# A decoder layer on one core: the embedding's projection moves from expert 19 to behind the last expert

## The chip, the cores and the metric

The kernel runs on one core of a Trainium2 chip. The metric is the device time of one execution in microseconds (us); the median of three runs is 1429.41 us (1429.36 to 1429.43).

## The reference, cut to what matters

One decoder layer on 512 tokens of width 1024, all in float32. A mixing sublayer is followed by a mixture of 32 experts, of which each token takes four, and by the part that the change is about: a per-layer embedding `p` of width 256 is projected to 1024, gated by a sigmoid of a 1024x1024 linear map of the residual, and added ahead of the last normalisation.

```python
x = layer_norm(DEEPNORM_ALPHA * x + ffn, ln2_g[i], ln2_b[i])          # ffn: the experts' output
gate = jax.nn.sigmoid((x @ ple_gate_w[i] + ple_gate_b[i]).astype(jnp.float32)).astype(x.dtype)
ple = p[i] @ ple_proj[i]
x = layer_norm(DEEPNORM_ALPHA * x + gate * ple, ln3_g[i], ln3_b[i])
```

`ple` depends on the inputs alone, so it can be computed at any time before the last loop.

## The kernel before

**Weights in chunks.** All weights pass through one list of chunks of 1 MB (`add`), in the order of use: for each expert eight chunks of its gate and up matrices, then four of the down matrix of the expert before. The chunk of `ple_proj` (`c_pp`) stands behind those of expert 19 (`EMBED + 1`), the four of `ple_gate_w` (`c_pg`) at the end. A ring of 14 buffers holds them. `load` brings a chunk into a free buffer by SP's queue; `split` makes two parts of it, a rounded one (`hi`, a cast on ScalarE, L114) and the rest (`lo`, a subtraction on VectorE, L117), so that each product is three matmuls (`mm3`, L210 to L212). `ahead(j)` says that chunk j is used: `done` gives its buffers back and loads what fits, `splits` splits the next chunks, up to three ahead of the one in use. `limit` says how far the list may be loaded; until the last expert it is two gate chunks short of the end.

**The experts.** The order of instructions on every engine is the order of the program text (it is written out by hand). In the loop over `e`, TensorE takes the eight chunks k = 0 to 7 of the expert (12 matmuls each), and then the four down chunks of the expert before (`down(e - 1)`), 12 each. Behind chunk 2 it transposes the hidden values of the expert before (`split_t`, L307), behind chunk 7 the gathered tokens of the next one. A transposition writes to a small PSUM buffer `tr`, of which there are two, taken in turn; ScalarE copies it out (L322) and VectorE subtracts (L323), and then the buffer is free again. `emit` scales the output and adds it to `acc` in DRAM by an indirect DMA from GpSimd (POOL), the scatter.

**Steps between chunks.** Generators are advanced behind given chunks: `embed_parts` in expert 19 behind chunks 1, 3, 4, 5 and 6 (first the two parts of the gate's bias, `pgb`, then for each of four tiles of `p` two transposes into a `tr` buffer, a copy on ScalarE and a subtraction on VectorE, L841 to L843), and `prepare` in expert 31 behind the same chunks (first the two parts of `b_down`, `bd`, then one transpose and one ScalarE copy for each tile, into `gt_`). `embed()` stands behind expert 19's down chunks: four tiles of 12 matmuls of 512 columns into `big`, a PSUM tile of which there are three, and a ScalarE copy of each to `ple[i]` (L853).

**The end.** Behind the last expert's `down`, whose output is halved between ScalarE and VectorE (L351, L352), come the remaining splits, 10 matmuls that only keep TensorE busy (`keep_warm`), and a loop of further blocks for experts with more than 96 tokens (`further_blocks`). It runs zero times here, but at its head all engines wait until each of them and the scatter are done (L768). Then SP loads the sum from `acc` (L999), two `combine` tiles add the experts' bias (L1011), 14 more `keep_warm` matmuls run, and for each of four tiles of tokens there is a normalisation (`second`), a transposition (`turn2`), the gate (`gate`, L1035 to L1042), the product with `ple` and the last normalisation.

Of the kernel before, what the change touches and what calls it, by code (L numbers as in the profile page):

```python
# [20 lines left out]
P = 128  # L21
S = 512
# [17 lines left out]
WARM_START, WARM_ROUTE, WARM_TURN, WARM_END = (6, 7, 7), (2, 2, 2), (3, 9), (10, 14)  # L40
# [8 lines left out]
def tile_layer(ctx: ExitStack, tc: tile.TileContext, x, p, w_in, pool_mix, pool_scale, conv_w, w_out,  # L49
# [42 lines left out]
    def give(*bs):  # L92
        for b in bs:
            (extra if type(b) is tuple else free if b < RING else late).append(b)
# [55 lines left out]
    def done(j, queue=nc.sync):  # L150

        give(*owned.pop(j))
        used[0] = j + 1
        fill(queue)

# [10 lines left out]
    def ahead(j):  # L166
        done(j)
        splits()

# [20 lines left out]
    for e in range(E):  # L190
        add_gu(e)
        if e:
            add_dn(e - 1)
        if e == EMBED + 1:
            c_pp = add(ple_proj[0].rearrange("(k p) c -> p k c", p=P), (2, 1024))
    add_dn(E - 1)
    last_more, last_split = c_gu[EMBED - 3][0], c_gu[EMBED - 2][0]
# [4 lines left out]
    def keep_warm(n, a, b):  # L202

        o = big()[:, 0, :b.shape[-1]]
        for _ in range(n):
            nc.tensor.matmul(o, a, b, start=True, stop=True)  # L206
# [638 lines left out]
    def embed():  # L845
        wh, wl = parts.pop(c_pp)
        for i in range(NT):
            o = big()
            for n in range(2):
                ns = slice(n * 512, (n + 1) * 512)  # L850
                for k in range(2):
                    mm3(o[:, n], ph[:, i, k], pl[:, i, k], wh[:, k, ns], wl[:, k, ns], k == 0, k == 1)
            nc.scalar.copy(ple[i], o.rearrange("p a b -> p (a b)"))  # L853
        ahead(c_pp)
# [41 lines left out]
    steps = iter(())  # L896
    for e in range(E):
# [7 lines left out]
        for k in range(ND):  # L905
# [4 lines left out]
            if k < ND - 1 or e:  # L910
                ahead(c_gu[e][k])
# [9 lines left out]
            if k == 1:  # L921
                steps = (tables(2, mp1) if e == 0 else tables(0, mp1) if e == 1 else
                         tables(e + 2, mp1) if e % 2 == 0 and e + 2 < E else
                         further() if e == 5 else prepare() if e == E - 1 else iter(()))
            if k in ((1, 2, 4) if e < E - 1 else (1, 3, 4, 5, 6)):
                next(steps, None)
            if e == EMBED + 1:
                if k == 1:
                    embed_steps = embed_parts()
                if k in (1, 3, 4, 5, 6):  # L930
                    next(embed_steps, None)
# [20 lines left out]
        if last:  # L952
            down(e - 1, {0: [finish, finish, finish]}, {3: [last_turn]})
            limit[0] = len(chunks)
            fill(nc.gpsimd)
        elif e:
            down(e - 1, {0: [multiply], 1: [gather_next], 2: [finish]})
        else:
            multiply()
            gather_next()  # L960
            finish()
# [16 lines left out]
        if e == EMBED + 1:  # L978
            embed()
            g3, b3 = spare_tiles[3][:, 0], spare_tiles[3][:, 1]  # L980
            gt_ = at("gt", RING + 2, F32R, S)
            bd = at("bd", RING + 1, F32R, D, D)[:96]

            for k in range(3):
                nc.gpsimd.dma_start(b3[32 * k:32 * k + 32], b_down[0])
    down(E - 1)
    lookahead[0] = 4
    splits(len(chunks) - nsplit[0] - 1)
    last_part = split(later=True)
    keep_warm(WARM_END[0], bsp[:, :P], bsp[:, :512])  # L990
# [12 lines left out]
    work3, _ = take(F32, free)  # L1003
    work3 = [work3[:, :512], work3[:, 512:D]]
# [54 lines left out]
    keep_warm(WARM_END[1], bsp[:, :P], bsp[:, :512])  # L1059
    last_part()  # L1060
    second(0)
    turn2(0)
# [47 lines left out]
```

## Time and profile before

| | |
|---|---|
| median of three runs | 1429.41 us (1429.36 to 1429.43) |
| the profiled execution's own time | 1432.01 us |
| its span, first to last instruction | 1430.2 us |
| TensorE busy (matmuls) | 1396.6 us, 98% |
| VectorE busy | 1235.9 us, 86% |
| ScalarE busy | 950.5 us, 66% |
| GpSimd busy | 446.9 us, 31% |
| DMA, mean over the span | 325 GB/s |

The times in the rows below are of the profiled execution, counted from its first instruction. PE is TensorE's matmuls, DVE VectorE, ACT ScalarE, POOL GpSimd, SP SyncE; SPq is an instruction of SP's queue. L853 is line 853 of the kernel. A matmul's end is modelled, so that two that follow each other overlap in the list; the distance of their starts is the pace.

### The profile page before, as it was taken

Reading aid. Unit: us, or ns where it says so; the run is one execution under the profiler, and the core shown is the slowest. Engines: PE = TensorE matmul, PEld = TensorE weight load, DVE = VectorE, ACT = ScalarE, POOL = GpSimd, SP = SyncE. Lnnn points to the kernel's source line nnn. Section 1 sums busy time; section 2 is a strip of 40 time slices with the busy share of each in tenths; the row PEclk is TensorE's granted clock in tenths of the full one; section 3 lists DMA queues with packets and bytes.
Section 4 is the critical chain, followed back from the end, with each engine's and each line's share of the span. In section 5 each row is a group of like instructions: output and inputs, shape, how many; then the busy total and the mean of one; then the engine's idle time right before and its main releaser. Section 6 shows DMA issues by size and latency. Waiting matters only on the chain.

```text
span 1430.2 us, 17695 instructions
## 1 busy us (share of the span) xinstructions
PE 1396.6 (98%) x6630; PEld 998.2 (70%) x6630; DVE 1235.9 (86%) x1049; ACT 950.5 (66%) x741; POOL 446.9 (31%) x203
## 2 busy tenths in 40 slices
PE   9999999999999999999999999999999999999796
PEld 8788766666666666666666666766666666666575
DVE  7645589999999999999989998799999999998775
ACT  5321367777777777777777776677777777777531
POOL 1101134455455555555532322122222222221100
PEclk9999999999999999999999999999999999999999
DMA  9327899999999999999989999899999999999321
GB/s 331 118 88 236 324 345 346 368 390 379 360 374 388 371 381 361 388 373 353 330 294 357 385 397 349 295 376 366 373 376 379 370 377 376 376 370 338 95 91 44
DMA packets 98071, 464.43 MB, mean 325 GB/s; under 512 B 9424, under 2 KB 19168, under 8 KB 65216
## 3 DMA queue, kind: packets, MB, share of 16 engines
q1 hardware_dynamic: 86240, 426.02, 77.6%
q0 software_dynamic: 10080, 35.53, 9.7%
q10 hardware_dynamic: 1664, 1.72, 0.5%
q8 instruction: 54, 0.88, 0.3%
q14 instruction: 33, 0.27, 0.0%
HBM read 443.97 MB, written 19.27 MB: 324 GB/s over the span
## 4 chain that ended last, share of the span: by engine, by line
PE 87%; DVE 6%; issue 4%; DMA 1%; ACT 1%; POOL 0%; SPq 0%; DVEq 0%; ACTq 0%; POOLq 0%
PE big L210 26%; PE big L212 25%; PE big L211 25%; PE tr L307 4%; PE big L1038 3%; DVE ring7dt.float32r L117 1%; PE big L903 1%; DVE ring8dt.float32r L117 1%; DVE ring10dt.float32r L117 1%; DVE ring6dt.float32r L117 1%; DVE ring2dt.float32r L117 1%; DMA acc<-yo,idxs 0%; PE big L206 0%; DMA x<-acc 0%; PE tr L569 0%
## 5 line engine op out<-in xcount | busy, mean ns | idle before, releaser
L339 POOL TENSOR_SCALAR h<-h 96x1024 f32<-96x1024 f32 x31 | 39.7, 1282 | 580.3 <-ACT h L338 580.3
L355 POOL DMA_INDIRECT acc<-yo,idxs x32 | 177.5, 5547 | 92.3 <-ACT yo L354 87.0
L212 PE MATMUL big<-chunk,xh 128*96 128x512 f32 x480 | 189.2, 394 | 0.0
L211 PE MATMUL big<-chunk,xl 128*96 128x512 f32 x480 | 188.5, 393 | 0.0
L345 POOL TENSOR_TENSOR gm<-gm,sg 96x1024 f32<-96x1024 f32 x31 | 104.1, 3357 | 65.8 <-ACT sg L344 64.0
L212 PE MATMUL big<-chunk,hh 128*96 128x512 f32 x268 | 105.5, 394 | 0.0
L211 PE MATMUL big<-chunk,hl 128*96 128x512 f32 x268 | 105.5, 394 | 0.0
L212 PEld LDWEIGHTS big<-chunk,xh 128*96 128x96 f32 x480 | 77.1, 161 | 33.2
L211 PEld LDWEIGHTS big<-chunk,xl 128*96 128x96 f32 x480 | 77.4, 161 | 31.1
L313 POOL DMA_INDIRECT xg<-x1d,idxg x31 | 91.7, 2958 | 21.9 <-DVE idxg L653 13.7
L212 PEld LDWEIGHTS big<-chunk,hh 128*96 128x96 f32 x268 | 43.4, 162 | 19.2
L211 PEld LDWEIGHTS big<-chunk,hl 128*96 128x96 f32 x268 | 43.3, 162 | 17.6
L344 ACT ACTIVATE sg<-gm 96x1024 f32<-96x1024 f32 x32 | 34.0, 1062 | 17.9 <-DVE gm L335 14.8
L322 ACT CAST xh<-tr 128x384 fp32r<-128x384 f32 x64 | 27.5, 479 | 24.0 <-PE tr L307 24.0
L354 ACT ACTIVATE yo<-big,gs 96x1024 f32<-96x1024 f32 x31 | 34.4, 1110 | 10.9 <-PE big L212 10.9
L347 DVE SCALAR_TENSOR_TENSOR h<-h,gm 96x1024 f32<-96x1024 f32 x32 | 38.7, 1211 | 2.6 <-POOL gm L345 2.6
L117 DVE TENSOR_TENSOR ring5dt.float32r<-ring5dt.float,ring3dt.float32r 128x2048 fp32r<-128x2048 f32 x13 | 31.1, 2390 | 11.4 <-ACT ring3dt.float32r L114 11.4
L117 DVE TENSOR_TENSOR ring8dt.float32r<-ring8dt.float,ring11dt.float32r 128x2048 fp32r<-128x2048 f32 x14 | 34.7, 2478 | 6.1 <-ACT ring11dt.float32r L114 6.1
L335 DVE TENSOR_SCALAR gm<-big 96x1024 f32<-96x1024 f32 x32 | 38.7, 1210 | 0.0
L117 DVE TENSOR_TENSOR ring10dt.float32r<-ring10dt.float,ring12dt.float32r 128x2048 fp32r<-128x2048 f32 x14 | 34.7, 2482 | 4.1 <-ACT ring12dt.float32r L114 4.0
L117 DVE TENSOR_TENSOR ring2dt.float32r<-ring2dt.float,ring13dt.float32r 128x2048 fp32r<-128x2048 f32 x14 | 34.7, 2480 | 3.5 <-ACT ring13dt.float32r L114 3.5
L322 ACT CAST hh<-tr 128x384 fp32r<-128x384 f32 x62 | 26.5, 479 | 16.8 <-PE tr L307 16.8
(577 smaller groups left out, 4447.0 us busy)
## 6 DMA issues: line engine op xcount, KB each, us to landing
ring10dt.float<-in_w_gate_up_dram SPq DMA_DIRECT2D x18, 1024.0 KB, 6.7
ring2dt.float<-in_w_gate_up_dram SPq DMA_DIRECT2D x18, 1024.0 KB, 7.8
ring3dt.float<-in_w_gate_up_dram SPq DMA_DIRECT2D x18, 1024.0 KB, 7.5
ring4dt.float<-in_w_gate_up_dram SPq DMA_DIRECT2D x18, 1024.0 KB, 7.6
ring9dt.float<-in_w_gate_up_dram SPq DMA_DIRECT2D x18, 1024.0 KB, 7.2
ring13dt.float<-in_w_gate_up_dram SPq DMA_DIRECT2D x17, 1024.0 KB, 7.0
ring1dt.float<-in_w_gate_up_dram SPq DMA_DIRECT2D x17, 1024.0 KB, 7.4
ring5dt.float<-in_w_gate_up_dram SPq DMA_DIRECT2D x17, 1024.0 KB, 6.5
```

The source lines that it names most:

```text
L117: second()
L210: nc.tensor.matmul(o, ah, bl, start=start, stop=False)
L211: nc.tensor.matmul(o, al, bh, start=False, stop=False)
L212: nc.tensor.matmul(o, ah, bh, start=False, stop=stop)
L307: nc.tensor.transpose(t[:, k, :], src[:, (4 * h + k) * P:(4 * h + k + 1) * P], ident[:n, :n])
L313: nc.gpsimd.indirect_dma_start(out=xg, out_offset=None, in_=x1d, in_offset=bass.IndirectOffsetOnAxis(ap=idxg[:, e:e + 1], axis=0))
L322: nc.scalar.copy(hi[:, 4 * h:4 * h + 4], t)
L335: nc.vector.tensor_scalar(gm, gp, LIMIT, None, op0=ALU.min)
L339: mul.tensor_scalar(h, h, LIMIT, -LIMIT, op0=ALU.min, op1=ALU.max)
L345: mul.tensor_mul(gm, gm, sg)
L355: nc.gpsimd.indirect_dma_start(out=acc, out_offset=bass.IndirectOffsetOnAxis(ap=idx, axis=0), in_=y, in_offset=None, compute_op=ALU.add)
L1038: nc.tensor.matmul(o, q[a + k // 4][:, k % 4], ws[k // 2][b][:, k % 2, c0:c1], start=False, stop=b == 1 and k == ND - 1)
```

## The change

The chunk of `ple_proj` moves behind the last expert's chunks. `embed()` becomes `embed(i)`, the matmuls of one tile, and `embedded(i, o)`, the copy of its result. Tiles 0, 1 and 2 stand directly behind the last expert's down matmuls, where 10 keep-warm matmuls were; tile 2's copy is halved between ScalarE and VectorE. Tile 3 stands behind the loop, between the two `combine` tiles and the keep-warm matmuls, which are 10 instead of 14. The steps of `embed_parts` move to chunks 0, 1, 4 and 5 of expert 19 and chunk 0 of expert 20, those of `prepare` to chunks 0, 1, 4, 5 and 6 of expert 31. Because the two parts of `p` (`ph`, `pl`) are needed until the end, `gt_` can't lie in their buffer any more: one buffer of expert 31's chunk 0 is kept for it and for `work3`. The last two gate chunks load from SP's queue as buffers come free in `down(30)`, no longer from GpSimd's behind it; one subtraction in the last expert's `down` stands behind its output (`later`).

```diff
-        if e == EMBED + 1:
-            c_pp = add(ple_proj[0].rearrange("(k p) c -> p k c", p=P), (2, 1024))
     add_dn(E - 1)
+    c_pp = add(ple_proj[0].rearrange("(k p) c -> p k c", p=P), (2, 1024))
...
-    def embed():
-        wh, wl = parts.pop(c_pp)
-        for i in range(NT):
-            o = big()
-            for n in range(2):
-                ns = slice(n * 512, (n + 1) * 512)
-                for k in range(2):
-                    mm3(o[:, n], ph[:, i, k], pl[:, i, k], wh[:, k, ns], wl[:, k, ns], k == 0, k == 1)
+    def embed(i):
+
+        wh, wl = parts[c_pp]
+        o = big()
+        for n in range(2):
+            ns = slice(n * 512, (n + 1) * 512)
+            for k in range(2):
+                mm3(o[:, n], ph[:, i, k], pl[:, i, k], wh[:, k, ns], wl[:, k, ns], k == 0, k == 1)
+        return o
+
+    def embedded(i, o, halves=False):
+        if halves:
+            nc.scalar.copy(ple[i][:, :512], o[:, 0])
+            nc.vector.tensor_copy(ple[i][:, 512:], o[:, 1])
+        else:
             nc.scalar.copy(ple[i], o.rearrange("p a b -> p (a b)"))
-        ahead(c_pp)
...
             if k < ND - 1 or e:
-                ahead(c_gu[e][k])
+                kept = ahead(c_gu[e][k], int(e == E - 1 and k == 0))
+            if kept:
+
+                (after_b,), kept = kept, ()
+                gt_ = at("gt", after_b, F32R, S)
...
-            if k == 1:
+            if k == (0 if e == E - 1 else 1):
                 steps = (tables(2, mp1) if e == 0 else tables(0, mp1) if e == 1 else
                          tables(e + 2, mp1) if e % 2 == 0 and e + 2 < E else
                          further() if e == 5 else prepare() if e == E - 1 else iter(()))
-            if k in ((1, 2, 4) if e < E - 1 else (1, 3, 4, 5, 6)):
+            if k in ((1, 2, 4) if e < E - 1 else (0, 1, 4, 5, 6)):
                 next(steps, None)
-            if e == EMBED + 1:
-                if k == 1:
-                    embed_steps = embed_parts()
-                if k in (1, 3, 4, 5, 6):
-                    next(embed_steps, None)
+            if (e, k) == (EMBED + 1, 0):
+                embed_steps = embed_parts()
+            if (e, k) in ((EMBED + 1, 0), (EMBED + 1, 1), (EMBED + 1, 4), (EMBED + 1, 5), (EMBED + 2, 0)):
+                next(embed_steps, None)
...
         if last:
+            limit[0] = len(chunks)
             down(e - 1, {0: [finish, finish, finish]}, {3: [last_turn]})
-            limit[0] = len(chunks)
-            fill(nc.gpsimd)
...
         if e == EMBED + 1:
-            embed()
             g3, b3 = spare_tiles[3][:, 0], spare_tiles[3][:, 1]
-            gt_ = at("gt", RING + 2, F32R, S)
...
-    down(E - 1)
-    lookahead[0] = 4
-    splits(len(chunks) - nsplit[0] - 1)
+    later = []
+    down(E - 1, {2: [lambda: later.append(split(later=True))]})
+    later[0]()
+    lookahead[0] = 5
+    splits(1)
+    embedded(0, embed(0))
+    o1, o2 = embed(1), embed(2)
     last_part = split(later=True)
-    keep_warm(WARM_END[0], bsp[:, :P], bsp[:, :512])
+    embedded(1, o1)
+    embedded(2, o2, True)
...
-    work3, _ = take(F32, free)
-    work3 = [work3[:, :512], work3[:, 512:D]]
+    work3 = [at(f"work3{k}", after_b, F32, 512, 512 * (k + 1)) for k in range(2)]
...
     combine(0)
     combine(1)
-    keep_warm(WARM_END[1], bsp[:, :P], bsp[:, :512])
+    o3 = embed(3)
+    keep_warm(WARM_END, bsp[:, :P], bsp[:, :512], tr([P, 512]))
     last_part()
     second(0)
+    embedded(3, o3)
+    parts.pop(c_pp)
+    done(c_pp)
     turn2(0)
```

## Rows read from the trace of the kernel before

**Rows 1.** The page's part 4: share of the chain that ended last, by engine.

```profile
PE 87%; DVE 6%; issue 4%; DMA 1%; ACT 1%; POOL 0%; SPq 0%; DVEq 0%; ACTq 0%; POOLq 0%
```

**Rows 2.** Stages: us; busy PE, PEld, DVE, ACT, POOL; clock, DMA share, GB/s.

```profile
847.60:900.10 52.50, 49.54 (x221) 35.19 (x220) 41.65 (x27) 34.93 (x29) 16.52 (x9) 0.97 0.93 326
936.00:1007.60 71.60, 71.35 (x337) 49.56 (x336) 66.64 (x46) 54.15 (x39) 17.86 (x9) 1.00 0.99 368
1186.70:1258.40 71.70, 71.44 (x339) 49.58 (x338) 66.72 (x46) 54.20 (x39) 17.92 (x9) 1.00 1.00 375
```

**Rows 3.** Timeline behind the last expert: start, us, engine, line [idle before <-releaser].

```profile
1346.35 0.69 ACT L351 ACTIVATE yo<-big,gs 96x512 f32<-96x512 f32 x1 [2.78 <-PE big L212]
1347.07 0.75 DVE L352 TENSOR_SCALAR yo<-big,gs 96x512 f32<-96x512 f32 x1 [0.39 <-ACT yo L351]
1349.68 1.90 ACT L114 CAST ring1dt.float32r<-ring9dt.float 128x2048 fp32r<-128x2048 f32 x1 [2.65 <-DMA ring9dt.float<-in_ple_gate_w_dram]
...
1355.78 2.47 SPq L999 DMA_DIRECT2D x<-acc  x5
1356.46 2.08 PE L1011 MATMUL big<-bd,gt 96*128 96x512 f32 x4 [7.89 <-issue]
1364.52 1.32 PE L307 MATMUL tr<-ident,x 128*128 128x128 f32 x8 [1.18 <-DVE x L298]
```

**Rows 4.** Timeline of TensorE: the first and the last of the projection's 48 matmuls.

```profile
889.03 0.47 PE L210 MATMUL big<-ring3dt.float32r,p 128*128 128x512 f32 x1
...
899.80 0.39 PE L212 MATMUL big<-ring10dt.float32r,p 128*128 128x512 f32 x1
```

**Rows 5.** Timeline of VectorE in expert 19.

```profile
853.85 2.28 DVE L117 TENSOR_TENSOR ring6dt.float32r<-ring6dt.float,ring9dt.float32r 128x2048 fp32r<-128x2048 f32 x1
...
858.36 1.22 DVE L836 TENSOR_TENSOR pgb<-after,pgb 32x1024 fp32r<-32x1024 f32 x1
859.61 2.29 DVE L117 TENSOR_TENSOR ring7dt.float32r<-ring7dt.float,ring0dt.float32r 128x2048 fp32r<-128x2048 f32 x1
861.82 1.01 DVE L323 TENSOR_TENSOR hl<-tr,hh 128x384 fp32r<-128x384 f32 x2
...
864.95 0.41 DVE L843 TENSOR_TENSOR p<-tr,p 128x256 fp32r<-128x256 f32 x1
...
903.08 2.29 DVE L117 TENSOR_TENSOR ring5dt.float32r<-ring5dt.float,ring3dt.float32r 128x2048 fp32r<-128x2048 f32 x1 [8.61 <-ACT ring3dt.float32r L114]
```

**Rows 6.** Timeline of TensorE in expert 19, at its two waits.

```profile
856.85 0.82 PE L307 MATMUL tr<-ident,h 96*128 96x96 f32 x8
...
862.42 0.44 PE L841 MATMUL tr<-ident,after 128*128 128x128 f32 x2 [1.97 <-DVE hl L323]
862.62 0.48 PE L210 MATMUL big<-ring11dt.float32r,xh 128*96 128x512 f32 x1
...
867.03 0.38 PE L841 MATMUL tr<-ident,after 128*128 128x128 f32 x2
...
877.38 0.55 PE L307 MATMUL tr<-ident,xg 96*128 96x96 f32 x4 [0.86 <-DVE p L843]
```

**Rows 7.** Stage table of TensorE alone (busy, clock, DMA): behind two waits.

```profile
863.30:866.70 3.40, 3.40 (x10) 0.53 1.01 428
...
1309.00:1313.00 4.00, 4.00 (x20) 1.00 0.89 357
```

**Rows 8.** Timeline in expert 31: VectorE's bd, TensorE's wait.

```profile
1304.72 1.22 DVE L889 TENSOR_TENSOR bd<-after,bd 32x1024 fp32r<-32x1024 f32 x1
...
1306.41 0.39 PE L212 MATMUL big<-ring7dt.float32r,xh 128*96 128x512 f32 x1
1308.78 0.32 PE L893 MATMUL tr<-ident,gsp 128*96 128x128 f32 x1 [1.99 <-DVE hl L323]
```

**Rows 9.** The chain of waits in order of time: the last scatter.

```profile
1348.10 6.72 DMA acc<-yo,idxs
```

**Rows 10.** Line 853: the projection's copies (min/median/max ns).

```profile
L853 ACT COPY after<-big x4: 1016/1016/1016, 892.1 to 900.2; 128x1024 f32<-128x1024 f32 x4
```

More of the change, by code (lines that the diff above doesn't have):

```diff
@@ L38 @@
 RING = 14
-WARM_START, WARM_ROUTE, WARM_TURN, WARM_END = (6, 7, 7), (2, 2, 2), (3, 9), (10, 14)
+WARM_START, WARM_ROUTE, WARM_TURN, WARM_END = (6, 7, 7), (2, 2, 2), (3, 9), 10
 TURN1 = 5
@@ L148, in fill, with done @@
                 break
-    def done(j, queue=nc.sync):
-        give(*owned.pop(j))
+    def done(j, queue=nc.sync, keep=0):
+        bs = owned.pop(j)
+        give(*bs[keep:])
         used[0] = j + 1
         fill(queue)
+        return bs[:keep]
     def splits(n=E):
@@ L164, in splits, with ahead @@
             fill()
-    def ahead(j):
-        done(j)
+    def ahead(j, keep=0):
+        kept = done(j, keep=keep)
         splits()
+        return kept
     def more(*bs, queue=nc.sync):
@@ L200, in tile_layer, with keep_warm @@
     c_pg = [add(wg[:, 2 * j:2 * j + 2, :], (2, 1024)) for j in range(4)]
-    def keep_warm(n, a, b):
-        o = big()[:, 0, :b.shape[-1]]
+    def keep_warm(n, a, b, o=None):
+        o = big()[:, 0, :b.shape[-1]] if o is None else o
         for _ in range(n):
@@ L894, in prepare @@
             nc.scalar.copy(gt_[:96, i * P:(i + 1) * P], gt)
-    steps = iter(())
+    steps, kept = iter(()), ()
     for e in range(E):
```

## The prediction

> **What bounds the kernel now.** I read the chain of waits first, then the stage table, then the instruction timelines of the places that the change touches. The chain puts 87% of the span on TensorE [rows 1]. The stage table says the same of the experts: in two ordinary experts (21 and 22) TensorE is busy 71.35 of 71.60 us, and VectorE 66.64 [rows 2]. So what TensorE issues among the experts costs its own time, unless a wait lies there anyhow; and a VectorE that is 93% full has a queue, which TensorE meets where it needs a buffer that VectorE is to free. Expert 19, which holds the embedding, lasts 52.5 us where two ordinary ones last 71.6 [rows 2]. Behind the last expert it is the other way round: TensorE stands still for 7.89 us, since everything waits for the last scatter [rows 3].
>
> **The projection leaves expert 19.** Its 48 matmuls run without a gap from 889.03 on [rows 4], until the next expert begins at 900.1 [rows 2]: 11.09 us, all on the path. VectorE is idle for 8.61 us of it [rows 5], so they hide nothing. What is late next when they go? VectorE: its gap was spare time. But experts 21, 22, 28 and 29 run without such a gap at 71.6 to 71.7 us a pair [rows 2], so the ordinary pace needs none. Gain 11.09.
>
> **The four transposes of p move to chunks 0, 1, 4, 5 and to chunk 0 of expert 20** (chunk 0 for pgb, the bias). Before, two waits come from them. The first: the transpose at chunk 3 takes the older of the two small PSUM buffers, which the expert's own transposes at chunk 2 filled; VectorE frees it with the subtraction that starts at 861.82, behind pgb's 1.22 us [rows 5]. TensorE is out of work at 860.45 and goes on at 862.42: 1.97 us [rows 6]. Behind that the clock is granted at 0.53, about the lower of its two levels, 1.2 GHz [rows 7], and the chunk that starts at 862.62 lasts until 867.03: 4.41 us, where its 12 matmuls take 2.8 at the 0.23 us of [rows 4]; so 1.6 us more. The second wait is 0.86 us at 877.38, for the last p subtraction [rows 6].
>
> After the change the order is: p's first transposes at chunk 1, the expert's own at chunk 2. The third taker of a two-buffer pool now is the second half of the expert's transposes, and it waits for p's subtraction. I follow VectorE's queue, which has no pause here [rows 5]: the subtraction at 853.85 ends at 856.13; pgb's comes right behind it (1.22 us) and ends at 857.4; the next chunk's, 2.25 us from start to start, ends at 859.65; p's, 0.41 us, at about 860.05. TensorE is there at 856.85 [rows 6] plus 0.14 for p's two transposes plus half of its own eight, 0.3: 857.3. It waits until about 860.1: 2.8 us in place of 1.97. So this wait is not removed; it moves one chunk ahead and grows by 0.85 us. The slow chunk behind it I keep at 1.6 us (nothing, below: the first rival). The second wait goes, since p's third subtraction then has two chunks, 5.6 us, to end; with the switch behind it that is 1.0 us. The fourth transpose costs its 0.14 us in expert 20 instead, and its subtraction joins VectorE's queue where it is full: 0 to 0.3 us there. Expert 19 in sum: -11.09 + 0.85 - 1.0 = -11.2, or -10.9 with the 0.3.
>
> **prepare() a chunk earlier in expert 31.** The same mechanism costs 1.99 us at 1308.78: bd's subtraction (1.22 us) stands in VectorE's queue ahead of the expert's own, for whose buffer the gate transpose at chunk 3 waits [rows 8]. After the change the gate transpose stands at chunk 1, and ScalarE alone frees its buffer (one copy, no subtraction). bd's subtraction comes a chunk earlier, ahead of a subtraction that was done at 1304.72 and then is at 1305.9; TensorE needs that one at 1306.6, behind its matmul at 1306.41 [rows 8]. So the wait goes with nothing late in its place: -2.1 with the switch. Keeping one buffer of chunk 0 costs the ring one load ahead of many; by the free list each of the last loads is still issued several chunks of 2.8 us before its split. I cost it at nothing; the cover is that lead, and without it ScalarE's casts would wait for a DMA, 1 to 3 us.
>
> **Behind the last expert.** 36 of the 48 matmuls take the place of 10 filling ones, from about 1346.15 on. At 0.229 us from start to start ([rows 4], 47 steps) they last 8.2 us and end at 1354.55. Meanwhile the scatter that all wait for lands 6.72 us after 1348.10, at 1354.82 [rows 9]; the three tiles lie in its shadow with 0.3 us over. The copies of tiles 0 and 1 (1.02 us each, [rows 10]) go between ScalarE's two last casts of 1.90 us [rows 3] and end by 1353.1. Tile 2 is halved as the last expert's output is: 0.69 us on ScalarE, 0.75 on VectorE [rows 3]. If the halves run side by side both end at about 1355.4, and the loop, which lets nobody pass until all have arrived, lets SP on some 0.3 us later: its first load of acc at 1356.1 instead of 1355.78. If VectorE waits for ScalarE's half, as the output's did (1347.07, behind 1346.35 + 0.69, [rows 3]), it is 0.75 us more. I take the first, since ple's halves are separate pieces that nothing reads yet: +0.3, bounds 0 and 1.1. That the last gate chunks now come by SP as buffers come free, and not by POOL behind expert 30, spares ScalarE its wait ahead of the cast at 1349.68 [rows 3], but not on the path, as the scatter ends last: 0.
>
> Behind the loop: 4 + 12 + 10 matmuls, 6.0 us at the upper level, between 1356.8 and the first transposes, at 1364.52 before [rows 3] and then at 1364.8, when VectorE has the first normalised tile. Tile 3's copy on ScalarE (1.02 us) lies between the square of the first tile and the copies of its transposes, which wait for these transposes. Nothing for either. The gates that follow are as before.
>
> **Sum.** -11.2 - 2.1 + 0.3 = -13.0 us. The profiled execution took 1432.01 us (span 1430.2, and 1.8 around it), so 1419.0 with a profile; the runs without one have a median of 1429.41, 2.6 us lower, and I take the difference over to them: 1416.4.
>
> A rule of the Trainium skill bears on both waits. The rows: behind 1.97 us of waiting the clock fell [rows 6, 7], behind 1.99 us at 1308.78 it stayed at 1.00 [rows 7, 8]. The Trainium skill's page "TensorE: Matmul & The Clock Gate", section "HAM oscillation — how this bites in real kernels", warns only of idle gaps longer than any in these experts. By that rule no wait here touches the clock, and the sum would be the first rival's; the first of the two rows disagrees.
>
> **Rivals.**
> 1. The clock stays up behind the longer wait in expert 19, as it did at 1308.78. Then 1.6 us more is gained: 1414.8. For it: one of two like waits. Against: the wait is longer now. If p's subtraction also comes so early that no wait is left, 2.8 us go as well: 1412.0.
> 2. The clock falls behind the loop. TensorE has two waits there, about 2.1 us at the loop and about 2 us ahead of the first transposes (1.18 before, [rows 3]). Behind the first, the filling matmuls absorb it; behind the second stand the gates, one after the other on the path: +1.6, so 1418, and with the halves one behind the other 1418.7.
> 3. The projection isn't hidden behind the last expert: the cover is only 0.3 us. If its matmuls went at the lower level (4.41 / 12 = 0.37 us and more each; at 0.43, 15.5 us in all), TensorE would reach the loop at 1361.7 and the end would move by 7 us: 1423. Against: TensorE is busy without a gap up to 1346.3.
> 4. It ends slower: VectorE becomes the bound of experts 20 to 30, since the gap in which it caught up is gone. It would cost 11 experts the amount by which VectorE's work exceeds TensorE's; slower from 13.0 / 11 = 1.2 us an expert, that is 74.0 us of VectorE work a pair. Against: it has 66.64 [rows 2]. At 75 us a pair, 1.7 us an expert, the time would be 1435.
>
> **Chances.** Forecast (1415 to 1417.6) 0.52, first rival 0.20, second 0.18, third 0.05, fourth 0.03, and 0.02 for no change, the gain going elsewhere. The range takes in the first two rivals, but not the first one's second step: 1413.0 to 1419.0. A change under 0.2% (2.9 us) is not told from none; faster 0.95, same 0.02, slower 0.03.
>
> **What would show it.** In the trace of the changed kernel: expert 19 as long as an ordinary one plus about 5 us, with one wait of TensorE near 2.8 us at its own transposes, ended by p's subtraction, and the 0.86 us wait gone; no wait at the gate transposes in expert 31; 36 matmuls directly behind the last expert's, and the first load of acc within 1.1 us of where it was, counted from the last expert's end. Wrong if experts 20 to 30 are longer than 71.7 us a pair, if the wait in expert 19 is gone or over 4 us, or if the stretch from the last expert's end (1346.3) to the end of the span, now 83.9 us, grows by more than 2 us.

## The result, and the profile after

The changed kernel takes 1420.01 us (median of 4 runs, 1419.95 to 1421.16), the kernel before beside it 1429.42 (4 runs, 1429.36 to 1430.57): ratio 0.9930 [0.9918, 0.9943], 9.4 us faster. Forecast were 1416.4 and a range of 1413.0 to 1419.0; the time lies 3.6 us above the one and 1.0 above the other. On a second chip, with 5 runs against 15, it was 1419.88 against 1430.80, ratio 0.9927 [0.9914, 0.9941].

The profiled execution of after took 1419.95 us, its span is 1418.1. Cut at the first matmul of each expert and at the first copy of the last expert's output, the two traces compare like this (us; the column "forecast" holds the prediction's terms):

| stretch | before | after | forecast | measured |
|---|---|---|---|---|
| start to expert 19 | 847.61 | 847.61 | 0 | 0 |
| expert 19 | 52.51 | 40.60 | -11.2 | -11.9 |
| expert 20 | 35.85 | 36.21 | 0 to 0.3 | +0.36 |
| experts 21 to 30 | 358.01 | 358.05 | 0 | 0 |
| expert 31 to its output's first copy | 52.36 | 50.18 | -2.1 | -2.2 |
| from there to the end | 83.87 | 85.51 | +0.3 | +1.6 |
| span | 1430.2 | 1418.1 | -13.0 | -12.1 |

The chain by engine is what it was [rows 1]:

```profile
PE 88%; DVE 6%; issue 4%; DMA 1%; ACT 1%; POOL 0%; DVEq 0%; SPq 0%; ACTq 0%; POOLq 0%
```

The stage table of after for expert 19, experts 21 and 22, 28 and 29 (columns as in [rows 2]):

```profile
847.60:888.20 40.60, 37.93 (x171) 26.23 (x170) 34.73 (x23) 28.85 (x24) 8.98 (x5) 0.96 0.98 362
924.40:996.10 71.70, 71.44 (x337) 49.59 (x336) 66.71 (x46) 54.22 (x39) 17.93 (x9) 1.00 1.00 372
1174.90:1246.60 71.70, 71.42 (x338) 49.57 (x336) 66.75 (x46) 54.22 (x39) 17.92 (x9) 1.00 1.00 374
```

Expert 19 has lost the projection's 48 matmuls but is still 4.75 us longer than an ordinary expert (71.70 / 2 = 35.85). The ordinary experts are unchanged: VectorE needed no gap to catch up in, so the fourth rival is out. VectorE in expert 19 of after [rows 5]:

```profile
853.85 2.28 DVE L117 TENSOR_TENSOR ring6dt.float32r<-ring6dt.float,ring9dt.float32r 128x2048 fp32r<-128x2048 f32 x1
856.16 1.22 DVE L838 TENSOR_TENSOR pgb<-after,pgb 32x1024 fp32r<-32x1024 f32 x1
857.41 2.29 DVE L117 TENSOR_TENSOR ring11dt.float32r<-ring11dt.float,ring5dt.float32r 128x2048 fp32r<-128x2048 f32 x1
859.62 0.42 DVE L845 TENSOR_TENSOR p<-tr,p 128x256 fp32r<-128x256 f32 x1
```

The forecast had these four at 853.85, 856.13, 857.4 and 859.65, the last one ending at 860.05. TensorE of the same stretch goes on right there [rows 6], and its clock falls behind the wait as before [rows 7]; the second fence is the stage table of TensorE alone:

```profile
857.07 0.49 PE L309 MATMUL tr<-ident,h 96*128 96x96 f32 x4
860.09 0.55 PE L309 MATMUL tr<-ident,h 96*128 96x96 f32 x4 [2.53 <-DVE p L845]
```

```profile
861.00:864.40 3.40, 3.40 (x10) 0.50 1.03 433
```

The wait is 2.53 us, forecast 2.8. The 0.86 us wait at the end of the expert is gone. In expert 31 [rows 8] bd's subtraction stands a chunk earlier on VectorE and the gate transpose waits for nothing; first VectorE's timeline, then TensorE's, whose first and third line here are gate transposes:

```profile
1290.98 1.22 DVE L897 TENSOR_TENSOR bd<-after,bd 32x1024 fp32r<-32x1024 f32 x1
...
1296.64 1.02 DVE L325 TENSOR_TENSOR hl<-tr,hh 128x384 fp32r<-128x384 f32 x2
```

```profile
1288.89 0.27 PE L901 MATMUL tr<-ident,gsp 128*96 128x128 f32 x1
...
1291.77 0.82 PE L309 MATMUL tr<-ident,h 96*128 96x96 f32 x8
...
1297.99 0.27 PE L901 MATMUL tr<-ident,gsp 128*96 128x128 f32 x1
```

The loss is behind the last expert. The timeline of after there [rows 3]; the projection's 36 matmuls, which start from 1332.43 to 1340.37, and ScalarE's casts and whole copies are left out:

```profile
1332.63 0.69 ACT L353 ACTIVATE yo<-big,gs 96x512 f32<-96x512 f32 x1 [0.97 <-PE big L214]
...
1333.36 0.75 DVE L354 TENSOR_SCALAR yo<-big,gs 96x512 f32<-96x512 f32 x1 [0.38 <-ACT yo L353]
1334.03 2.28 DVE L996 TENSOR_TENSOR ring10dt.float32r<-ring10dt.float,ring9dt.float32r 128x2048 fp32r<-128x2048 f32 x1
1334.38 5.42 POOL L357 DMA_INDIRECT acc<-yo,idxs  x1 [6.91 <-DVE yo L354]
...
1336.22 2.28 DVE L117 TENSOR_TENSOR ring1dt.float32r<-ring1dt.float,ring11dt.float32r 128x2048 fp32r<-128x2048 f32 x1
...
1340.79 0.59 ACT L859 COPY after<-big 128x512 f32<-128x512 f32 x1 [1.70 <-PE big L214]
1341.41 0.69 DVE L860 COPY after<-big 128x512 f32<-128x512 f32 x1 [2.91 <-ACT after L859]
1344.46 2.30 SPq L1012 DMA_DIRECT2D x<-acc  x5
1345.06 1.53 PE L1023 MATMUL big<-bd,gt 96*128 96x512 f32 x4 [4.30 <-issue]
```

and the chain of waits [rows 9]:

```profile
1334.38 9.23 DMA acc<-yo,idxs
```

The scatter starts where it did, 1.75 us behind the output's first copy. But GpSimd's instruction takes 5.42 us, where it took 1.56, and its data lands after 9.23 us instead of 6.72. It begins while VectorE is in a subtraction, and a second one follows without a pause; it ends at 1339.80, 1.3 us behind the end of the second, about as long as the instruction takes by itself. The first load of acc is 11.83 us behind the output's first copy, 9.43 before: 2.4 us later, where the prediction's own sign was at most 1.1. In front of the loop, tile 2's VectorE half waits for ScalarE's half, as the output's does.

### The profile page after: what moved, and what is told of

The parts are those of the page before. It is cut to its first block, busy times and chain, and to the rows that moved or that the text cites. A ratio compares the mean times of both kernels' runs of the same rounds, so it can differ in the third digit from the quotient of the medians.

```text
span 1418.1 us, 17667 instructions
## 1 busy us (share of the span) xinstructions
PE 1390.6 (98%) x6616; PEld 994.3 (70%) x6616; DVE 1235.8 (87%) x1050; ACT 949.6 (67%) x741; POOL 446.4 (31%) x201
## 4 chain that ended last, share of the span: by engine, by line
PE 88%; DVE 6%; issue 4%; DMA 1%; ACT 1%; POOL 0%; DVEq 0%; SPq 0%; ACTq 0%; POOLq 0%
PE big L212 27%; PE big L214 26%; PE big L213 26%; PE tr L309 4%; PE big L1050 3%; DVE ring11dt.float32r L117 1%; PE big L911 1%; DMA acc<-yo,idxs 1%; DVE ring0dt.float32r L117 1%; DVE ring1dt.float32r L117 1%; DVE ring13dt.float32r L117 1%; DVE ring3dt.float32r L117 1%; DVE ring12dt.float32r L117 1%; DMA xs<-in_x_dram 0%; PE tr L571 0%
## 5 line engine op out<-in xcount | busy, mean ns | idle before, releaser
L347 POOL TENSOR_TENSOR gm<-gm,sg 96x1024 f32<-96x1024 f32 x31 | 103.7, 3346 | 65.8 <-ACT sg L346 64.0
L117 DVE TENSOR_TENSOR ring12dt.float32r<-ring12dt.float,ring6dt.float32r 128x2048 fp32r<-128x2048 f32 x14 | 35.3, 2521 | 7.8 <-ACT ring6dt.float32r L114 7.8
L356 ACT ACTIVATE yo<-big,gs 96x1024 f32<-96x1024 f32 x31 | 34.5, 1111 | 10.9 <-PE big L214 10.9
L117 DVE TENSOR_TENSOR ring9dt.float32r<-ring9dt.float,ring2dt.float32r 128x2048 fp32r<-128x2048 f32 x14 | 34.7, 2481 | 4.3 <-ACT ring2dt.float32r L114 4.3
L117 DVE TENSOR_TENSOR ring3dt.float32r<-ring3dt.float,ring10dt.float32r 128x2048 fp32r<-128x2048 f32 x14 | 34.7, 2481 | 4.0 <-ACT ring10dt.float32r L114 4.0
L117 DVE TENSOR_TENSOR ring1dt.float32r<-ring1dt.float,ring8dt.float32r 128x2048 fp32r<-128x2048 f32 x14 | 34.7, 2481 | 3.7 <-ACT ring8dt.float32r L114 3.7
```

Of the source, the lines that this page charges most:

```text
L117: second()
L347: mul.tensor_mul(gm, gm, sg)
```

## The experiments

There are three sets of four, each on one chip beside runs of the kernel before. Times in a fence are of that run's one trace. "The stretch behind" is the time from the output's first copy to the end of the span: 83.87 us in the trace of before, 85.51 after.

**The kernel before, unchanged.**

> The kernel before, unchanged. Its profiled execution took 1432.01 us, 2.6 more than the median of its other runs, and the prediction carried that difference over to the changed kernel, whose profiled execution took no more than its other runs. Theory A (the 2.6 us were that one execution's own): a second profiled execution takes 1429.3 to 1429.6, and its trace is shorter than the first at one or two places, the slow chunk behind the first wait of expert 19 (1.6 us) among them. Theory B (a profile costs this kernel 2.6 us): 1432 again, with the same stages as the first trace.

Median 1430.58 us (1428.65 to 1433.67, 10 runs), ratio 0.9998 [0.9988, 1.0007]; the 21 runs beside it 1427.90 to 1433.35. In this trace the clock fell behind both of the 2 us waits, in the first trace of before only behind that of expert 19; the stage table of TensorE alone, behind the gate transposes' wait of 1.99 us:

```profile
1309.20:1312.60 3.40, 3.40 (x10) 0.50 0.81 331
```

Expert 31 took 53.93 us up to its output, 1.57 more than in the first trace. The profiled execution took 1433.67 us, the longest of the ten and 3.1 above their median: theory A's 1429.3 to 1429.6 did not come. Nor did theory B, since the stages differ, and runs beside it without a trace took up to 1433.35; the part on why the prediction was wrong comes back to this. So runs of this kernel spread over 5.8 us, and the three runs of 1429.4 at the start were a sample from the lower half: over the 57 runs of before, on four occasions, the median is 1430.6.

**One subtraction behind the output, in the kernel before.**

> The kernel before, with one thing of the change alone: the subtraction of the second gate chunk stands behind the last expert's output instead of ahead of it, so that it runs on VectorE while GpSimd issues the last scatter. Theory A (a VectorE subtraction of two SBUF operands keeps GpSimd from issuing the scatter): GpSimd's instruction lasts 3.0 to 3.6 us instead of 1.56, the scatter lands 8.2 to 8.8 us after its start instead of 6.72, and the time is 1.5 to 2 us longer, near 1431. Theory B (in the changed kernel the scatter is late for another reason, TensorE's matmuls beside it or the transfers): 1.6 us for the instruction, and no change of the time (within 0.3 us).

```diff
-    down(E - 1)
+    later = []
+    down(E - 1, {2: [lambda: later.append(split(later=True))]}, {2: [lambda: lookahead.__setitem__(0, 2)]})
+    later[0]()
```

Median 1432.21 (1429.92 to 1434.48, 11 runs), ratio 1.0014 [1.0005, 1.0023]. Its timeline, VectorE and GpSimd:

```profile
1347.96 2.28 DVE L988 TENSOR_TENSOR ring13dt.float32r<-ring13dt.float,ring0dt.float32r 128x2048 fp32r<-128x2048 f32 x1
1348.33 3.35 POOL L355 DMA_INDIRECT acc<-yo,idxs  x1 [5.28 <-DVE yo L352]
```

The instruction grew from 1.56 to 3.35 us and ended 1.44 us behind the subtraction: that part is as theory A said. The landing grew only from 6.72 to 7.09 us, not to 8.2, and the stretch behind was 83.80. So in this trace the 1.8 us at the issue cost nothing. The times say otherwise: the median rose by 2.1 us (0.7 to 3.3 by the interval), about as much as theory A forecast. Where the runs without a trace lost it isn't known, so what one subtraction costs stays open.

**The changed kernel with the scatter's issue free.**

> The changed kernel, in which VectorE first copies half of the projection's tile 0 (it waits for its matmuls) and only then runs the two subtractions of the gate chunks; all else as it is. Theory A (subtractions beside the scatter's issue): GpSimd's instruction falls from 5.42 us to 1.6 to 2.3, the first load of acc is issued 9.5 to 9.9 us after the last expert's last matmul instead of 11.87, and the time falls by 1.9 to 2.4 us, to 1417.6 to 1418.1. Theory B (another reason): 5 us and more again for the instruction, 1420.0. Theory C (the loads behind the loop take up the rest): the scatter is as in A, but the time falls by under 1 us.

```diff
-    later[0]()
...
-    splits(1)
-    embedded(0, embed(0))
+    o0, second2 = embed(0), split(later=True)
+    embedded(0, o0, True)
+    later[0]()
+    second2()
```

Median 1419.17 (1416.51 to 1422.13, 5 runs), ratio 0.9923 [0.9907, 0.9939]. VectorE now first copies half of tile 0, for which it has to wait, and the scatter goes out in that pause (the timeline without TensorE's rows):

```profile
1331.61 0.75 DVE L354 TENSOR_SCALAR yo<-big,gs 96x512 f32<-96x512 f32 x1 [0.39 <-ACT yo L353]
1332.64 1.43 POOL L357 DMA_INDIRECT acc<-yo,idxs  x1 [6.91 <-DVE yo L354]
...
1334.26 0.69 DVE L860 COPY after<-big 128x512 f32<-128x512 f32 x1 [1.90 <-ACT after L859]
1334.86 2.28 DVE L999 TENSOR_TENSOR ring10dt.float32r<-ring10dt.float,ring9dt.float32r 128x2048 fp32r<-128x2048 f32 x1
1337.06 2.29 DVE L1000 TENSOR_TENSOR ring1dt.float32r<-ring1dt.float,ring11dt.float32r 128x2048 fp32r<-128x2048 f32 x1
1339.69 0.69 DVE L860 COPY after<-big 128x512 f32<-128x512 f32 x1 [0.35 <-ACT after L859]
1341.20 0.83 SPq L1013 DMA_DIRECT2D x<-acc  x2
```

5.42 us became 1.43 with the same work in another order, as theory A said, and theory B is out; acc's load moved from +11.8 to +10.3, the stretch behind to 83.81. Last now is tile 2's second half (1339.69). The time does not decide between theories A and C: the median is 0.7 to 0.8 us under the changed kernel's two, and the five runs spread over 5.6 us.

**The steps of p spread out.**

> The changed kernel, with the steps of p elsewhere: pgb behind chunk 4 of expert 19, the four tiles of p behind chunk 5 of experts 19, 21, 23 and 25, where VectorE has caught up. Theory A (the wait of 2.5 us in expert 19 and the slow clock behind it come from p's subtraction between VectorE's others): no wait of TensorE over 0.5 us in expert 19, the expert 36.0 us long instead of 40.6, and the time 1415.3 to 1416. If the clock's fall behind the wait isn't in the timed executions, 1417. Theory B (VectorE is behind there in any case, and the wait moves on to another place): an expert 19 of 38 us and more, or longer experts 20 to 25, and the time 1418 or more.

```diff
-            if (e, k) == (EMBED + 1, 0):
+            if (e, k) == (EMBED + 1, 4):
                 embed_steps = embed_parts()
-            if (e, k) in ((EMBED + 1, 0), (EMBED + 1, 1), (EMBED + 1, 4), (EMBED + 1, 5), (EMBED + 2, 0)):
+            if (e, k) in ((EMBED + 1, 4), (EMBED + 1, 5), (EMBED + 3, 5), (EMBED + 5, 5), (EMBED + 7, 5)):
```

Median 1416.53 (1416.00 to 1417.07, 4 runs), ratio 0.9901 [0.9886, 0.9916]: theory A, though 0.5 us above its 1415.3 to 1416. Expert 19 lasts 35.87 us, without a wait of TensorE and without a fall of its clock; experts 21, 23 and 25 are 0.22 longer each. That is 3.4 us under the changed kernel's median of 1419.9 to 1420.0 (other chips), by the order of the same instructions alone.

**prepare() alone.**

> The kernel before, of the whole change only the moved steps of prepare() in expert 31. Theory A (the wait at the gate transposes goes and nothing comes in its place): from expert 31's start to its output's first copy 50.2 us instead of 52.4 in the first trace of before, no TensorE wait near 1308.8, median 2.0 to 3.0 us under the kernel before run beside it (2.2 for the wait and its switch, up to 0.8 more as the clock can no longer fall behind it, which it did in one of two traces of before and cost 1.6). Rival B (the wait is taken over by the expert's own transposes, as happened in expert 19): 51.5 to 52.4 us there and under 1 us gained.

```diff
-            if k == 1:
+            if k == (0 if e == E - 1 else 1):
...
-            if k in ((1, 2, 4) if e < E - 1 else (1, 3, 4, 5, 6)):
+            if k in ((1, 2, 4) if e < E - 1 else (0, 1, 4, 5, 6)):
```

Median 1428.06 (1425.34 to 1429.46, 11 runs) against 1430.80, ratio 0.9984 [0.9975, 0.9993]. Expert 31 took 50.19 us and has no wait: theory A. Not expected: in this trace the scatter landed after 5.9 us and acc's load started 0.85 us sooner behind the output (+8.58), and the stretch behind was 81.57.

**The changed kernel again.**

> The changed kernel as it is, beside the others on one chip. Theory A (its runs differ by whether the clock falls behind the 2.5 us wait in expert 19 and behind the loop, 1.5 us each): runs spread over 1416.5 to 1421, median 1418 to 1420, ratio to before 0.992 to 0.993, that is 10 to 11.5 us. Rival B (the first four runs were typical and before is what varies): median 1420.0 with under 1 us of spread.

Median 1419.88 (1417.97 to 1421.24, 5 runs). The trace has the same wait, 2.52 us, and this time no fall of the clock behind it (the stage table of TensorE alone), so expert 19 took 39.05 us instead of 40.60:

```profile
860.80:864.20 3.40, 3.40 (x17) 1.00 1.01 428
```

So the clock's fall behind a wait of this size is a matter of the run, and the runs spread over 3.3 us: theory A.

**Both edits.**

> The changed kernel with both edits: half of tile 0's copy ahead of the two subtractions behind the last expert, and the steps of p spread over experts 19, 21, 23 and 25. Theory A (the two losses are separate): expert 19 in 35.9 us, scatter's instruction 1.4 to 1.6 us, the stretch from the output's first copy to the end of the span 83.8, median 1413.8 to 1415.0, which is 1.6 to 2.7 us under the changed kernel with p spread alone (1416.5). Rival B (that stretch is set by tile 2's two halves, so the scatter's 1.5 us come back only in part): 1415.5 to 1416.5.

Median 1415.19 (1413.97 to 1417.20, 4 runs), ratio 0.9898 [0.9882, 0.9913]; the stretch behind 84.68. 4.7 us under the changed kernel beside it. On the border between the two theories, and no proof by itself of the scatter's share, since the kernel with p spread alone ran on another chip; both came again below.

**The kernel before without its waits.** The projection stays in expert 19.

> The kernel before, the projection left in expert 19, but prepare()'s steps moved as in the change, and the steps of p moved to chunks 4 and 5 of expert 18 and 4, 5 and 6 of expert 19. Theory A (the waits of about 2 us in experts 19 and 31 are what lets runs of before differ, by the clock's fall behind them): both waits gone, the 0.86 us one kept, expert 19 in 48.5 to 49.0 us instead of 52.5, runs within 1.5 us of each other, median 1423.8 to 1426. Rival B (the spread comes from elsewhere, from the end or the start): the same two waits gone, but the runs are spread over 4 us or more as those of before. Either way the difference to the changed kernel with p spread (1416.5) is what the projection itself is worth once its steps wait for nothing: 11.09 less the 1.6 lost at the scatter, 9.5, by A 1426.0.

```diff
-            if e == EMBED + 1:
-                if k == 1:
-                    embed_steps = embed_parts()
-                if k in (1, 3, 4, 5, 6):
-                    next(embed_steps, None)
+            if (e, k) == (EMBED, 4):
+                embed_steps = embed_parts()
+            if (e, k) in ((EMBED, 4), (EMBED, 5), (EMBED + 1, 4), (EMBED + 1, 5), (EMBED + 1, 6)):
+                next(embed_steps, None)
```

with prepare() as above. Median 1424.71 (1424.59 to 1425.61, 5 runs), ratio 0.9963 [0.9949, 0.9976]. The five runs lie within 1.0 us, where 15 runs of before beside them spread over 5.3, as theory A said. But the waits are not all that lets runs differ: the other kernels here that have neither of them, with four runs each, spread over 1.1 us (p spread), 3.1 (the same again), 3.2 and 3.3 (both edits, twice). With the two waits of 2 us gone, expert 19 keeps the clock and the projection (stage table, columns as in [rows 2]):

```profile
847.60:896.60 49.00, 47.54 (x220) 34.16 (x220) 40.65 (x25) 33.72 (x27) 17.43 (x9) 1.00 0.96 349
```

So 6.1 us, where the whole change gained 10.9 on this chip, are to be had without moving the projection. And moving it, with p's steps out of the way, is worth 1424.71 - 1416.53 = 8.2 us (two chips), not 9.5: the stretch behind was 82.53 here and 85.62 to 86.98 in the two traces with p spread, so 3.1 to 4.5 us were lost there and not 1.6.

**With p spread, again.**

> The changed kernel with the steps of p spread, the scatter's instruction still held up (5.4 us), again, as the base of the next three. Theory A (the loss at the scatter is 1.6 us or more of time, as the traces have it): 1.4 to 2.4 us above the kernel with both edits beside it. Rival B (what the loop gives back, the gates lose: the transposes, not acc's load, set the end): within 0.7 us of it, as the two ratios to before of the two earlier chips have it (0.9901 and 0.9898).

Median 1416.29 (1416.06 to 1419.16, 4 runs).

**Both edits, again, on the same chip.**

> The kernel with both edits again. Theory A: 1414.0 to 1415.3, 1.4 to 2.4 us under the kernel with p spread alone. Rival B: within 0.7 us of it.

Median 1414.19 (1413.82 to 1417.09, 4 runs), ratio 0.9886 [0.9870, 0.9903]: 2.1 us under the run above. In the traces the stretch behind went from 85.62 to 84.00. This is what theory A said, but each set has one run 3 us above the others and the two intervals overlap, so the times alone don't prove it. It is the fastest version by the medians: 5.8 us under the changed kernel's 1420.01 (other chip).

**Tile 2 copied whole.**

> Both edits, and tile 2 copied whole by ScalarE ahead of the loop (1.02 us) in place of its two halves, one behind the other (0.59 + 0.69 from first start to last end 1.31). Theory A (with the scatter free, tile 2's copy is what the loop waits for last): acc's first load 0.2 to 0.4 us earlier, counted from the output's first copy (10.0 instead of 10.3), and the time within 0.4 us of the kernel with both edits. Rival B (the scatter's landing is last, 5.4 us behind its start at +1.74): no change of acc's load.

```diff
-    embedded(2, o2, True)
+    embedded(2, o2)
```

acc's load came at +9.72 instead of +10.30: tile 2's copy did end last. Median 1415.17 (1413.64 to 1417.95, 4 runs), 1.0 us above the run before it where theory A allowed 0.4; the 0.6 us don't show in the time, and in this trace TensorE waited 2.29 us ahead of the first transposes.

**Two tiles ahead, two behind.**

> Both edits, and of the embedding's tiles two ahead of the loop and two behind it; the subtraction of the last gate chunk but one stands behind the loop, that of the last one behind the first tile's transposes; 4 filling matmuls instead of 10. Theory A (tile 2, not the scatter, ends last ahead of the loop once the scatter is free; behind the loop 4 + 24 + 4 matmuls of 0.23 us fit into the 7.4 to 8.8 us between acc's load and the first transposes): acc's first load 8.1 to 8.6 us behind the output's first copy instead of 10.3, the end at 81.5 to 83 instead of 84.7, median 1412.5 to 1414. Rival B (the wait at the loop, now longer for TensorE, costs the clock, or the third tile's buffer delays the fourth and the transposes): transposes at 18.5 or later, 1414.5 to 1416.

```diff
     o1 = embed(1)
     last_part = split(later=True)
     embedded(1, o1)
...
+    o2 = embed(2)
     combine(0)
     combine(1)
+    second2()
+    embedded(2, o2)
+    o3 = embed(3)
+    keep_warm(4, bsp[:, :P], bsp[:, :512], tr([P, 512]))
     second(0)
     embedded(3, o3)
...
     turn2(0)
+    last_part()
     second(1)
```

Median 1417.48 (1416.39 to 1418.64, 4 runs), ratio 0.9903 [0.9887, 0.9920]: slower than the version with three ahead. The first half of theory A held, acc's load came at +7.95; the rest was the fall of the clock that rival B named and one more thing, and the time lies above both forecasts. Its timeline (L1080 is `last_part`):

```profile
1336.08 2.56 SPq L1011 DMA_DIRECT2D x<-acc  x5
...
1336.67 0.56 PE L212 MATMUL big<-ring8dt.float32r,p 128*128 128x512 f32 x1 [3.11 <-issue]
...
1341.78 0.69 DVE L276 SCALAR_TENSOR_TENSOR x<-x,big 128x512 f32<-128x512 f32 x1 [3.01 <-PE big L1022]
...
1346.35 1.38 PE L309 MATMUL tr<-ident,x 128*128 128x128 f32 x8
...
1348.99 2.28 DVE L1080 TENSOR_TENSOR ring2dt.float32r<-ring2dt.float,ring3dt.float32r 128x2048 fp32r<-128x2048 f32 x1
...
1355.77 1.34 PE L309 MATMUL tr<-ident,x 128*128 128x128 f32 x8 [1.97 <-issue]
```

Tile 2 stood ahead of the combine matmuls, and the clock fell at 1337.0 as TensorE began it. So the first tile's sum in VectorE waited for its combine matmul (1341.78) and came 5.7 us behind acc's load, where it came 3.3 us behind in the version with three ahead; the first transposes gained 0.2 us in all. And the last subtraction now stands ahead of the second tile's normalisation: TensorE waited 1.97 us at the second transposes, with a fall of the clock behind it (1357.4), where the version with three ahead has no wait.

## Why the prediction was wrong in its size

**What held.** Expert 19 and expert 31. The first wait moved a chunk ahead and grew, the second one went, VectorE's queue came out within 0.1 us; -11.2 was forecast for experts 19 and 20, -11.5 came. prepare()'s wait went with nothing late in its place: -2.2 for -2.1. The ordinary experts didn't move. The third and fourth rivals didn't happen. One reading was wrong without consequence: VectorE's idle 8.61 us run from 894.47 to 903.08, and only 5.65 of them lie within the projection's 11.09.

**The step that failed in the trace: "+0.3" behind the last expert.** It measured +1.6. The prediction set the projection's matmuls against a scatter that "lands 6.72 us after", as if that were the scatter's own. It is a time with an issue in it, by GpSimd, and the change puts two subtractions of VectorE beside this issue. The experiments with one subtraction (3.35 us), two (5.42) and none (1.43) show that it is these. The prediction counted the order of VectorE's work as no cost, since nobody on VectorE's side waited. The trace of before had the sign. Its scatters, first those of 17 experts and then those of the other 15 (ns, shortest/median/longest):

```profile
L355 POOL DMA_INDIRECT acc<-yo,idxs x17: 1474/10923/11399, 241.7 to 814.4; - x17
```

```profile
L355 POOL DMA_INDIRECT acc<-yo,idxs x15: 1475/1491/4007, 850.5 to 1348.1; - x15
```

The median is 10.9 us in the first and 1.49 in the second: an operation of which one and the same form takes 1.5 or 11 us depends on something beside it, and a plan that moves things beside it has to ask on what. The same trace answers. A long scatter and a short one, with VectorE's rows beside them:

```profile
706.15 10.92 POOL L355 DMA_INDIRECT acc<-yo,idxs  x1 [1.69 <-ACT yo L354]
706.85 2.27 DVE L117 TENSOR_TENSOR ring1dt.float32r<-ring1dt.float,chunk 128x2048 fp32r<-128x2048 f32 x1
...
713.46 2.28 DVE L117 TENSOR_TENSOR ring4dt.float32r<-ring4dt.float,chunk 128x2048 fp32r<-128x2048 f32 x1
...
715.66 1.01 DVE L323 TENSOR_TENSOR hl<-tr,hh 128x384 fp32r<-128x384 f32 x2
```

```profile
1223.41 2.28 DVE L117 TENSOR_TENSOR ring1dt.float32r<-ring1dt.float,ring8dt.float32r 128x2048 fp32r<-128x2048 f32 x1
1225.55 1.48 POOL L355 DMA_INDIRECT acc<-yo,idxs  x1 [1.19 <-ACT yo L354]
1225.62 1.21 DVE L347 SCALAR_TENSOR_TENSOR h<-h,gm 96x1024 f32<-96x1024 f32 x1
```

The long one ends 1.33 us behind the last of four subtractions without a gap between them, the short one 1.34 us behind the subtraction in which it began, though VectorE goes on at once with another kind of instruction. The 14 traces hold 448 scatters. 439 of them had a subtraction beside them as they began, or one that began within 1.1 us; each ended 1.30 to 1.44 us behind the end of the last in that unbroken run (of `tensor_tensor` instructions whose inputs both lie in SBUF, nearly all of them these subtractions). The other nine took 1.43 to 1.56 us. So what counts is not that VectorE is busy but when the run of subtractions ends.

The Trainium skill's page "SBUF — State Buffer", section "Who interferes with whom", says that a VectorE instruction with two inputs in SBUF contends with a GpSimd instruction that reads SBUF, and that whichever starts first holds the shared ports. The 5.42 and 3.35 us agree in this: both times the subtraction had begun first. The section also reports a probe in which `tensor_tensor` did not stall a DMA; here it held up the issue of one. Nor does the rule account for all of it: L347, whose two inputs lie in SBUF as well, did not hold up the short scatters, and the long one above began 0.70 us before its first subtraction; why is not shown.

Added to this came the bound that the prediction named and didn't take: tile 2's halves ran one behind the other (1340.79 + 0.59, then 1341.41 + 0.69), so the upper bound of that term, 1.1, was nearer than 0.3. With the scatter late it cost nothing in the changed kernel (the half ended at 1342.10, the scatter landed at 1343.61); with the scatter free it was what the loop waited for.

Of the 2.4 us by which acc's load was late, 0.8 came back: TensorE was free of its wait ahead of the first transposes (1.18 us in [rows 3]), which started 1.9 us late, and the gates behind them lost 0.3 less. One trace on each side makes the loss look small. The four traces with the old order and no late subtraction (two of them with prepare() moved) have stretches behind of 81.57 to 84.24 us, the four with the changed order 85.51 to 86.98: 3.0 us apart in the mean, where 0.3 was forecast.

**The step that failed outside the trace: "2.6 us lower, and I take the difference over to them".** The profiled execution of before was 2.6 us above the median of three runs; that of after was at the median. Span against span the change is worth 12.1 us, run against run 9.4 on the first chip and 10.9 on the second. The other kernels speak against an offset that profiling adds: in the runs with one late subtraction and with prepare() moved, which are otherwise the kernel before, the profiled execution lies at the median (1432.20 and 1432.21; 1428.06 both). Runs of before differ, and they differ with the clock. Its 53 runs on the three later chips have a mean granted clock on record: the four at 0.995 took 1427.9 to 1428.7 us, the 14 at 0.994 1429.0 to 1430.5, the 22 at 0.993 1428.0 to 1433.4, the 13 at 0.992 and below 1430.2 to 1433.7. Two places for a fall are the waits of 2 us, about 1.6 us each time; falls in the stretch behind the last expert (10.2 us at the lower level in the first trace of before, 6.8 with prepare() moved) come on top. So the offset wasn't there to be taken over. 3.6 us were missed: 0.9 by the trace, 2.6 by this. That division holds for these two executions only: by the 57 runs the offset is 1.4, and by the four traces a side the loss behind the last expert is larger. Which of the falls the three runs at 1429.4 had isn't known, since they have no trace.

**The rivals.** The first, no fall of the clock behind the longer wait, came about in two of the three traces with this wait (39.05 and 39.06 us for expert 19). It is not one of two ways in which the kernel goes, but one of two in which a run goes. In the old order the clock fell behind expert 19's wait in all four traces that have it, behind expert 31's in one of three. The second rival's fall behind the loop is in the trace, 3.4 us at the lower level from 1345.7 on, but it was there before too (from 1351.6 to 1361.8, of which TensorE worked in 5.4) and is nearly all absorbed by the filling matmuls; the fall that would have cost, behind a wait ahead of the first transposes, didn't come, as that wait is gone in the trace of after.

## What to carry to other kernels

A transfer that is issued by GpSimd has two parts, and here the issue ended only behind VectorE's subtractions. Before work is put into the shadow of such a transfer, look at the shortest and the longest time of that instruction over the whole kernel, find what stands beside the long ones, and put a VectorE instruction that must wait anyway ahead of it. A difference between one profiled execution and the median of a few runs is not to be carried over to another kernel; take several traces on each side, and count a clock's fall behind a short wait as a chance in every run. A wait behind a full queue goes when its cause moves to where the queue is short: here the spread steps gave 3.4 us more.

## What the runs showed of the hardware

The clock of TensorE, at 2.4 GHz before, was granted at 0.50 to 0.53 for 3.4 us (the lower level, 1.2 GHz) behind waits of 1.97, 1.99 and 2.53 us in some runs, and stayed at 1.00 behind waits of 1.99 and 2.52 us at the same places in others. A scatter's instruction that takes 1.43 to 1.56 us by itself ended 1.30 to 1.44 us behind the end of the unbroken run of VectorE's subtractions that ran beside it, in 439 of 439 cases, as if it began only then. In the changed kernel the delay of the issue reached the landing whole: 5.42 us and 9.23, then 1.43 and 5.18 with the issue free. In the kernel before, 1.8 us more in the issue came with 0.4 more in the landing, which is not told from chance, since landings with an issue of 1.56 us lie between 5.61 and 6.79.
